# Layer 1's attention in groups of four heads, and six weight buffers instead of nine

## The chip, the cores and the metric

One core of a Trainium2 chip runs the whole program in one launch. The metric is device time in microseconds (us) of that core. Five engines work side by side, each through its own queue in order: TensorE (PE) for matrix products, VectorE (DVE), ScalarE (ACT), GpSimd (POOL), and SyncE (SP), which here issues the transfers from memory. PE writes its results to PSUM, of which the program uses eight banks: four under the name "acc" and four under the name "sc".

## The reference

A decoder of two layers over 256 tokens of 1024 numbers. Each layer adds an attention to its input and then a gated feed-forward part with a short convolution; all in float32, with a root-mean-square norm ahead of each.

```python
for i in range(DEPTH):                      # DEPTH = 2
    hn = rms_norm(h, norm_mix[i])
    if kind == 0:
        mix = moba_mixer(hn, a_w_qkv[j], a_w_o[j], cos_h, sin_h)
    elif kind == 1:
        mix = mla_mixer(hn, b_w_in[j], b_q_norm[j], b_w_uq[j], b_kv_norm[j], b_w_ukv[j], b_w_o[j], cos_r, sin_r)
...
    h = h + mix.astype(h.dtype)
    f = conv_ffn(rms_norm(h, norm_ffn[i]), ffn_w_gate[i], ffn_conv_w[i], ffn_conv_b[i], ffn_w_up[i], ffn_w_down[i])
    h = h + f.astype(h.dtype)
return rms_norm(h, norm_final)
```

Both attentions have 16 heads and are causal. With 256 tokens layer 0's is a plain softmax attention with 64 numbers a head. Layer 1's first makes small latents (384 and 256 numbers), and from them, for each head, a query and a key of 64 + 32 = 96 numbers (the last 32 rotated by position, and in the key shared by all heads) and a value of 64:

```python
s = jnp.einsum("bqhd,bkhd->bhqk", qi, k, preferred_element_type=jnp.float32) * scale
s = jnp.where(key_pos[None, :] <= qpos[:, None], s, NEG_INF)
p = jax.nn.softmax(s, axis=-1).astype(v.dtype)
return jnp.einsum("bhqk,bkhd->bqhd", p, v)
```

## The kernel before

**Weights.** All weights come in one stream of 186 units, in the order of use. A unit is up to 128 x 1152 numbers, mostly 128 x 1024. `load_unit` (L159) takes a room for the raw unit (pool `rawp`, five of them), has SP fetch it, and splits it into a high and a low part in two pieces of 512 columns: ACT casts `whi` (L173), DVE subtracts `wlo` = raw - whi (L174). The two parts lie in the pool `wp` (L125), which has nine buffers of each. `mm3` (L177) then makes each product of three matmuls, high x high, high x low, low x high (L178 to L180). A unit of 1024 columns feeds 24 matmuls of 256 columns. A buffer comes free when PE has done its last matmul with the unit; the cast for the unit nine further on waits for that, so nine is also how far ACT and DVE can work ahead of PE.

**Order.** Each engine works strictly in the order in which its instructions stand, and a program that builds the kernel sets that order: it may move instructions past each other according to when it expects buffers and results, so that the size of a pool changes the order too, at places that the code does not name.

**An attention in four groups.** Per group of four heads: the weights' products for q, k and v (the "filler", lists of small pieces of work that `run_fill` hands out), then for each head
- `products`: scores q x k into a bank "sc" (L279), two blocks of queries, of 128 and 256 keys;
- `exps`: DVE scales, masks and takes the row maxima from the bank (L293), ACT the exponentials with their sums (L296);
- `divide`: DVE's reciprocal (L304) and the division, on ACT (L307) or DVE (L309);
- `flip`: three transposes on PE into a bank "sc" (L316) and a copy `pT` of them;
- `values`: `pT` x v for a pair of heads, 64 columns of weights each, into a bank "sc" (L330), copied to `oh` on ACT (L332) and `ol` on DVE (L333).

**Layer 0** (`quads`, L351) does this for four heads at a time. Its heads have 2 x 32 rows, so the products of four heads run side by side in PE. In the stretch of a group stand the products and exponentials of its four heads, the transposes and values of the four before, and between them the filler for the next group, cut by shares of its length. Its tiles pb, pn, pT have four buffers each. The rotation of q and k is DVE's work (L569 to L571), q and k of a group before its products.

**Layer 1** (`run` and `slot`, L375 and L335) does it for two heads at a time, with a depth of two buffers: in slot p the values of pair p - 2, the products and softmax of pair p, the transposes of pair p - 1, with filler between. Here q is made with tokens in the rows (L776, and the rotation with DVE L251 and L253 and POOL L254), then flipped by four transposes per block of tokens (L807, with copies L808). The products have 96 rows. The divisions are DVE's, the copies `pT` ACT's for even heads and DVE's for odd ones.

**Feed-forward.** `ffn` (L419): for each pair of 128 columns, four units and 96 matmuls on PE; then `gate`, on DVE, ACT and POOL (from L438, ACT L442, gelu L447, POOL L448, to L451), beside the next pair's matmuls.

Of the kernel before, what the change touches and what calls it, by code (L numbers as in the profile page):

```python
# [10 lines left out]
F32 = mybir.dt.float32  # L11
# [5 lines left out]
P = 128  # L17
S = 256
NT = S // P
D = 1024  # L20
KD = D // P
H = 16
HD = 64
F = 2816
FC = F // P
QL, KVL, ROPE = 384, 256, 32
CQ, CKV = QL // P, KVL // P
DQK = HD + ROPE
G = 4
HG = H // G  # L30
# [90 lines left out]
def trunk(ctx: ExitStack, tc: tile.TileContext, xT, scalars, gfin, wstream, consts_in, out):  # L121
    nc = tc.nc
    const = ctx.enter_context(tc.tile_pool(name="const", bufs=1))
    rawp = ctx.enter_context(tc.tile_pool(name="rawp", bufs=5))
    wp = ctx.enter_context(tc.tile_pool(name="wp", bufs=9))  # L125
    act = ctx.enter_context(tc.tile_pool(name="act", bufs=1))
    sm = ctx.enter_context(tc.tile_pool(name="sm", bufs=4))
    ps = ctx.enter_context(tc.tile_pool(name="ps", bufs=1, space=PSUM))
# [62 lines left out]
    class SumSq:  # L191


        def __init__(self):
            self.acc = None
# [60 lines left out]
    def run_fill(fill, ns):  # L256
        while fill and ns > 0:
            cost, fn = fill.popleft()
            fn()
            ns -= cost  # L260
        return ns
# [3 lines left out]
    class Attention:  # L265


        def __init__(self, pool, scale, qT, kT, v, oh, ol, depth):
            self.pool, self.scale, self.qT, self.kT, self.v, self.oh, self.ol = pool, scale, qT, kT, v, oh, ol
            self.depth, self.sc, self.ex, self.pb, self.pT = depth, {}, {}, {}, {}  # L270

        def products(self, pair):
            sc = [ps.tile([P, 3 * P], F32, name="sc", bufs=4) for _ in pair]
            self.sc.update(zip(pair, sc))
            for t, (a, b) in enumerate(CUTS):
                parts = [list(zip(self.qT(n, t), self.kT(n, b - a))) for n in pair]
                for i in range(len(parts[0])):
                    for o, qk in zip(sc, parts):
                        nc.tensor.matmul(o[:, a:b], *qk[i], start=i == 0, stop=i == len(qk) - 1,  # L279
                                         skip_group_check=True)  # L280

        def softmax(self, n):
            self.exps(n)
            self.divide(n)

        def exps(self, n):
            sc = self.sc.pop(n)
# [12 lines left out]
        def divide(self, n):  # L300
            pb, rs = self.ex.pop(n)
            pn = self.pool.tile([P, 3 * P], F32, name="pn", bufs=self.depth)
            rc = sm.tile([P, NT], F32, name="rc")
            nc.vector.reciprocal(rc, rs)  # L304
            for t, (a, b) in enumerate(CUTS):
                if self.depth > 2:
                    nc.scalar.activation(pn[:, a:b], pb[:, a:b], AF.Copy, scale=rc[:, t:t + 1])  # L307
                else:
                    nc.vector.tensor_scalar(pn[:, a:b], pb[:, a:b], rc[:, t:t + 1], None, op0=ALU.mult)  # L309
            self.pb[n] = pn  # L310

        def flip(self, n):
            pb = self.pb.pop(n)
            pt = ps.tile([P, 3 * P], F32, name="sc", bufs=4)
            for b in range(3):
                nc.tensor.transpose(pt[:, b * P:(b + 1) * P], pb[:, b * P:(b + 1) * P], ident)  # L316
            pT = self.pool.tile([P, 3 * P], F32, name="pT", bufs=self.depth)
            if n % 2 == 0 or self.depth > 2:
                nc.scalar.copy(pT, pt)
            else:  # L320
                nc.vector.tensor_copy(pT, pt)
            self.pT[n] = pT

        def values(self, ns):
# [6 lines left out]
                                     start=t == 0, stop=t == NT - 1)  # L331
            nc.scalar.copy(self.oh[:, pr], o)  # L332
            nc.vector.tensor_sub(self.ol[:, pr], o, self.oh[:, pr].bitcast(F32))  # L333

        def slot(self, p, fill, ns):  # L335

            if p > 1:
                self.values((2 * p - 4, 2 * p - 3))
            if p < H // 2:
                pair = (2 * p, 2 * p + 1)  # L340
                self.products(pair)
                for n in pair:
                    self.softmax(n)
            left = run_fill(fill, ns * 0.4)
            if 0 < p <= H // 2:
                self.flip(2 * p - 2)
                left = run_fill(fill, left + ns * 0.2)
                self.flip(2 * p - 1)
                run_fill(fill, left + ns * 0.4)

        def quads(self, fill, next_fill):  # L351

            for g in range(G + 1):
# [17 lines left out]
                    self.values((n, n + 1))  # L371
                    run_fill(fill, ns * 0.1)
                run_fill(fill, 1e9)

        def run(self, fill, next_fill):  # L375
            for p in range(H // 2 + 2):
                if p and p % 2 == 0 and p < H // 2:
                    run_fill(fill, 1e9)
                    fill = next_fill(p // 2)
                slots = max(1, H // 2 + 1 - p) if p >= H // 2 - 2 else 2 - p % 2  # L380
                ns = sum(c for c, _ in fill) - (2600 if p >= H // 2 - 2 else 0)
                self.slot(p, fill, max(ns, 0) / slots)
            run_fill(fill, 1e9)

    def out_proj_fill(oh, ol, ks, accs):

# [171 lines left out]
    with tc.tile_pool(name="at0", bufs=1) as ap:  # L558
        ap.tile([P, 32], F32, name="pad")
        oh = ap.tile([P, KD, S], F32R, name="oh")  # L560
        ol = ap.tile([P, KD, S], F32R, name="ol")
# [64 lines left out]
        def group_fill(g):  # L626
            fill, us, box = deque(), [], {}

            def get(i):
                while len(us) <= i:  # L630
                    us.append(load_unit())
                return us[i]

            def qk(w, i, k):
                if i == 0 and k == 0:
                    box[w] = ps.tile([P, 2, S], F32, name="acc", bufs=4)
                wh, wl = get(2 * w + i)
                c = slice(k * P, (k + 1) * P)
                mm3(box[w][:, i], wh[:, c], wl[:, c], zh[:, k], zl[:, k], k == 0, k == KD - 1)
                if i == 1 and k == KD - 1:  # L640
                    evac_qk(g, w, box[w])

            def v(k, t):
                if k == 0 and t == 0:
                    box["v"] = ps.tile([P, NT, 256], F32, name="acc", bufs=4)
                mm_v(box["v"], get(4 + k // 4), k, t, k == 0)
                if k == KD - 1 and t == NT - 1:
                    evac_v(g, box["v"])

            for w in range(2):  # L650
                for i in range(2):
                    for k in range(KD):
                        fill.append((330, lambda w=w, i=i, k=k: qk(w, i, k)))
            for t in range(NT):
                for k in range(KD):
                    fill.append((330, lambda k=k, t=t: v(k, t)))
            return fill
# [11 lines left out]
        def v0(n, t):  # L669
            return vs[n // HG][:, t, n % HG]  # L670

        att = Attention(ap, HD ** -0.5, q0, k0, v0, oh, ol, HG)
        first_group()
        accs = []
        fill = group_fill(1)
        run_fill(fill, 5500)
        ks = {G - 1: range(4), G: range(4, KD - 2)}
# [10 lines left out]
    with tc.tile_pool(name="at1", bufs=1) as ap:  # L688
# [7 lines left out]
                c = slice(k * P, (k + 1) * P)  # L696
                mm3(dst, u[0][:, c], u[1][:, c], zh[:, k], zl[:, k], start and k == 0, k == KD - 1)

        tab = ap.tile([P, 3 * P], F32, name="pT", bufs=2)[:2 * ROPE, :S]
        nc.sync.dma_start(tab, consts_in[:2 * ROPE, CRT:])  # L700
        pkv = ps.tile([P, CKV, S], F32, name="acc", bufs=4)
        us = [load_unit() for _ in range(CKV)]
# [5 lines left out]
        for k in range(KD):  # L708
            c = slice(k * 2 * ROPE, (k + 1) * 2 * ROPE)
# [8 lines left out]
        for i in range(CQ):  # L718
            pq = ps.tile([P, S], F32, name="acc", bufs=4)
            mm_in(pq, load_unit(), range(KD), True)  # L720
            if i == 0:
                r2 = rstd_latent(ssk.columns(), KVL, r)
            if i == 1:
                R2 = rows_sb(r2)
                for j in range(CKV):
                    y = act.tile([P, S], F32, name="ssacc", bufs=2)
                    nc.vector.scalar_tensor_tensor(y, pkv[:, j], sc_in[:, GK + j:GK + j + 1], R2,
                                                   op0=ALU.mult, op1=ALU.mult)
                    nc.scalar.copy(ch[:, CQ + j], y)
                    nc.vector.tensor_sub(cl[:, CQ + j], y, ch[:, CQ + j].bitcast(F32))  # L730
                R0 = rows(r)
                tabR = ap.tile([P, 3 * P], F32, name="sb", bufs=2)[:2 * ROPE, :S]
                nc.vector.tensor_tensor(tabR, tab, R0[:2 * ROPE], op=ALU.mult)
                y = ap.tile([P, 3 * P], F32, name="pb", bufs=2)[:2 * ROPE, :S]
                nc.vector.tensor_tensor(y, pr[:2 * ROPE], tabR, op=ALU.mult)
                y2 = ap.tile([P, 3 * P], F32, name="pb", bufs=2)[:ROPE, :S]
                nc.scalar.copy(y2, y[ROPE:])
                nc.vector.tensor_tensor(kTs[0][HD:DQK], y[:ROPE, None, :].to_broadcast([ROPE, HG, S]),
                                        y2[:, None, :].to_broadcast([ROPE, HG, S]), op=ALU.add)
                nc.vector.tensor_copy(kTs[1][HD:DQK], kTs[0][HD:DQK])  # L740
            g = sc_in[:, GQ + i:GQ + i + 1]
            nc.scalar.activation(ch[:, i], pq, AF.Copy, scale=g)
            nc.vector.scalar_tensor_tensor(cl[:, i], pq, g, ch[:, i].bitcast(F32), op0=ALU.mult, op1=ALU.subtract)
            sqq = act.tile([P, 2, S], F32, name="sq", bufs=2)[:, 0]
            nc.scalar.activation(sqq, pq, AF.Square)
            ssq.add(sqq)
        oh = ap.tile([P, KD, S], F32R, name="oh")
# [76 lines left out]
        def v1(n, t):  # L824
            return vs[n // HG][:, t, n % HG]

        att = Attention(ap, DQK ** -0.5, q1, k1, v1, oh, ol, 2)
        ks, vv, qs, fl = group_fill(0)
        run_fill(deque(ks + vv), 1e9)
        r1 = rstd_latent(ssq.columns(), QL, r)  # L830
# [4 lines left out]
        accs = []  # L835
        fill = group_fill(1)
        for f in fl:
            run_fill(fill, 1000)
            f[1]()
        att.run(fill, lambda g: group_fill(g + 1) if g < G - 1 else out_proj_fill(oh, ol, range(KD - 2), accs))  # L840
        us = [load_unit() for _ in range(2)]
        zh, zl = new_z()
        ss = SumSq()
# [30 lines left out]
```

## Time and profile before

| | us |
|---|---|
| median of 3 runs | 590.43 |
| lowest and highest | 590.33, 590.66 |
| the profiled execution | 590.41 |
| its span, first to last instruction | 588.6 |
| PE busy | 575.8 |
| DVE busy | 421.2 |
| ACT busy | 355.9 |
| POOL busy | 50.6 |

The profile is one execution. A row of a timeline has the start in us from the span's start, the length, the engine, the line of the code, the operation, what it writes <- what it reads, its shape, and how many equal instructions stand in the row; in brackets, how long the engine stood idle before it, and what it had waited for. The length of PE's rows contains the way through the array; for the pace one reads start to start.

### The profile page before, as it was taken

How to read it: one execution, taken by the hardware profiler on the slowest of the kernel's cores; microseconds unless marked ns; L12 is line 12 of the kernel's file. 1: busy time of each engine (PE TensorE's matmuls, PEld its weight loads, DVE VectorE, ACT ScalarE, POOL GpSimd, SP SyncE). 2: the span in 40 equal slices, each digit the busy share in tenths (PEclk: the TensorE clock that was granted, in tenths of full speed). 3: DMA queues.
4: the chain of work that ended last, by engine and by line, in shares of the span. 5: the costliest groups of instructions: out<-in, count | busy, mean ns of one | idle time of the engine just before them, and what ended most of it. 6: DMA issues, size and time to landing. Idle time of an engine off the chain costs nothing.

```text
span 588.6 us, 12160 instructions
## 1 busy us (share of the span) xinstructions
PE 575.8 (98%) x4695; PEld 550.2 (93%) x4695; DVE 421.2 (72%) x908; ACT 355.9 (60%) x768; POOL 50.6 (9%) x47
## 2 busy tenths in 40 slices
PE   8998999999999999999999999999999999999995
PEld 7998999999999999999999888999999999988884
DVE  5898774595978778754488889658778778784403
ACT  6778778565656566544376677546657566573302
POOL 1000000001121211200002200000021211210001
PEclk9998999999999999999999999999999999999999
DMA  8667533535455656675636413255465656655101
GB/s 284 264 225 277 189 137 108 179 130 194 162 196 204 209 172 211 206 218 173 212 121 226 161 48 109 73 179 179 144 216 186 220 171 216 205 188 200 49 1 71
DMA packets 30074, 101.76 MB, mean 173 GB/s; under 512 B 3488, under 2 KB 4848, under 8 KB 30016
## 3 DMA queue, kind: packets, MB, share of 16 engines
q1 hardware_dynamic: 29744, 100.24, 50.5%
q8 instruction: 37, 0.61, 0.4%
q0 software_dynamic: 128, 0.48, 0.3%
q10 hardware_dynamic: 144, 0.26, 0.1%
q14 instruction: 21, 0.17, 0.1%
HBM read 99.92 MB, written 1.05 MB: 172 GB/s over the span
## 4 chain that ended last, share of the span: by engine, by line
PE 78%; issue 12%; DVE 4%; ACT 2%; DMA 2%; POOL 1%; SPq 0%; POOLq 0%; DVEq 0%; ACTq 0%
PE acc L178 19%; PE acc L179 19%; PE acc L180 19%; PE sc L179 5%; PE sc L178 5%; PE sc L180 5%; PE sc L279 3%; PE sc L330 2%; DVE wlo L174 2%; PE sc L316 2%; DMA raw<-in_wstream 2%; ACT whi L173 1%; PE sc L807 1%; ACT pb L296 0%; POOL r L216 0%
## 5 line engine op out<-in xcount | busy, mean ns | idle before, releaser
L174 DVE TENSOR_TENSOR wlo<-raw,whi 128x512 fp32r<-128x512 f32 (+1 forms) x371 | 239.9, 687 | 70.9 <-ACT whi L173 70.6
L173 ACT CAST whi<-raw 128x512 fp32r<-128x512 f32 (+1 forms) x371 | 209.9, 618 | 105.6 <-PE acc L180 43.4
L178 PE MATMUL acc<-zh,whi 128*128 128x256 f32 (+1 forms) x816 | 228.1, 280 | 0.3 <-ACT whi L173 0.3
L179 PE MATMUL acc<-zh,wlo 128*128 128x256 f32 (+1 forms) x816 | 226.5, 278 | 0.2 <-DVE wlo L174 0.2
L180 PE MATMUL acc<-zl,whi 128*128 128x256 f32 (+1 forms) x816 | 226.2, 277 | 0.0
L178 PEld LDWEIGHTS acc<-zh,whi 128*128 128x128 f32 (+1 forms) x816 | 153.5, 188 | 2.2 <-ACT whi L173 1.5
L179 PEld LDWEIGHTS acc<-zh,wlo 128*128 128x128 f32 (+1 forms) x816 | 153.5, 188 | 0.4 <-DVE wlo L174 0.4
L180 PEld LDWEIGHTS acc<-zl,whi 128*128 128x128 f32 (+1 forms) x816 | 153.3, 188 | 0.0
L448 POOL TENSOR_TENSOR gc<-gc,R 128x512 f32<-128x512 f32 x22 | 34.8, 1583 | 193.1 <-ACT gc L447 181.8
L178 PE MATMUL sc<-hh,whi 128*128 128x256 f32 x176 | 48.6, 276 | 0.0
L179 PE MATMUL sc<-hh,wlo 128*128 128x256 f32 x176 | 48.6, 276 | 0.0
L180 PE MATMUL sc<-hl,whi 128*128 128x256 f32 x176 | 48.6, 276 | 0.0
L450 ACT CAST hh<-gm 128x512 fp32r<-128x512 f32 x22 | 13.7, 621 | 44.1 <-DVE gm L449 44.1
L178 PE MATMUL acc<-oh,whi 128*128 128x256 f32 x128 | 38.0, 297 | 0.0
L179 PE MATMUL acc<-oh,wlo 128*128 128x256 f32 x128 | 36.0, 281 | 0.0
L180 PE MATMUL acc<-ol,whi 128*128 128x256 f32 x128 | 35.8, 280 | 0.0
L179 PE MATMUL sc<-whi,hl 128*128 128x512 f32 x88 | 34.6, 394 | 0.0
L178 PE MATMUL sc<-whi,hh 128*128 128x512 f32 x88 | 34.5, 393 | 0.0
L180 PE MATMUL sc<-wlo,hh 128*128 128x512 f32 x88 | 34.2, 389 | 0.0
L296 ACT ACTIVATE pb<-sb,nm 128x128 f32<-128x128 f32 x64 | 28.3, 445 | 8.5 <-DVE nm L293 8.5
L178 PEld LDWEIGHTS sc<-hh,whi 128*128 128x128 f32 x176 | 33.0, 188 | 0.0
L179 PEld LDWEIGHTS sc<-hh,wlo 128*128 128x128 f32 x176 | 33.0, 188 | 0.0
(143 smaller groups left out, 900.4 us busy)
## 6 DMA issues: line engine op xcount, KB each, us to landing
raw<-in_wstream SPq DMA_DIRECT2D x175, 512.0 KB, 4.1
raw<-in_wstream SPq DMA_DIRECT2D x13, 256.0 KB, 4.5
raw<-in_wstream SPq DMA_DIRECT2D x4, 576.0 KB, 3.7
h<-in_xT SPq DMA_DIRECT2D x8, 128.0 KB, 4.4
gl<-in_gfin SPq DMA_DIRECT2D x1, 512.0 KB, 3.7
out<-hn SPq DMA_DIRECT2D x1, 512.0 KB, 2.6
ropeR<-in_consts POOLq DMA_DIRECT2D x1, 384.0 KB, 4.4
out<-hn ACTq DMA_DIRECT2D x1, 256.0 KB, 2.7
```

The source lines that it names most:

```text
L173: nc.scalar.copy(hi[:, a:b], raw[:, a:b])
L174: nc.vector.tensor_sub(lo[:, a:b], raw[:, a:b], hi[:, a:b].bitcast(F32))
L178: nc.tensor.matmul(o, lh, rh, start=first, stop=False, skip_group_check=True)
L179: nc.tensor.matmul(o, ll, rh, start=False, stop=False, skip_group_check=True)
L180: nc.tensor.matmul(o, lh, rl, start=False, stop=last, skip_group_check=True)
L279: nc.tensor.matmul(o[:, a:b], *qk[i], start=i == 0, stop=i == len(qk) - 1, skip_group_check=True)
L296: nc.scalar.activation(pb[:, a:b], sb[:, a:b], AF.Exp, scale=-1.0, bias=nm[:, t:t + 1], accum_out=rs[:, t:t + 1])
L316: nc.tensor.transpose(pt[:, b * P:(b + 1) * P], pb[:, b * P:(b + 1) * P], ident)
L330: nc.tensor.matmul(o[j * HD:(j + 1) * HD, t * P:], self.v(n, t), pT[j][:, a:b], start=t == 0, stop=t == NT - 1)
L448: nc.gpsimd.tensor_tensor(gc, gc, Rb, op=ALU.mult)
L450: nc.scalar.copy(hh[:, f0:f0 + 2], gm)
L807: nc.tensor.transpose(pt[:DQK, i], st[g][:, t, i], ident)
```

## The change

`wp` goes from nine buffers to six. Layer 1's attention goes from `run` and `slot` to `quads`, so its products, exponentials, transposes, divisions and values come in fours as in layer 0, and its tiles pb, pn and pT get four buffers each, in the room of the three weight buffers. A new argument `on_act` keeps the divisions and copies on the engines that had them: ACT in layer 0, DVE (and ACT for even heads' copies) in layer 1. The filler of the last two stretches is the output product's first four and next two units instead of six in one list. `softmax`, `slot` and `run` go. Each engine has as many instructions as before. Line numbers of the new file are one higher up to the attention and lower behind it.

```diff
-    wp = ctx.enter_context(tc.tile_pool(name="wp", bufs=9))
+
+    wp = ctx.enter_context(tc.tile_pool(name="wp", bufs=6))
...
-        def __init__(self, pool, scale, qT, kT, v, oh, ol, depth):
+        def __init__(self, pool, scale, qT, kT, v, oh, ol, depth, on_act):
...
-                if self.depth > 2:
+                if self.on_act:
                     nc.scalar.activation(pn[:, a:b], pb[:, a:b], AF.Copy, scale=rc[:, t:t + 1])
...
-            if n % 2 == 0 or self.depth > 2:
+            if n % 2 == 0 or self.on_act:
                 nc.scalar.copy(pT, pt)
...
-        tab = ap.tile([P, 3 * P], F32, name="pT", bufs=2)[:2 * ROPE, :S]
+        tab = ap.tile([P, 3 * P], F32, name="pT", bufs=HG)[:2 * ROPE, :S]
...
-        att = Attention(ap, DQK ** -0.5, q1, k1, v1, oh, ol, 2)
+        att = Attention(ap, DQK ** -0.5, q1, k1, v1, oh, ol, HG, False)
...
-        att.run(fill, lambda g: group_fill(g + 1) if g < G - 1 else out_proj_fill(oh, ol, range(KD - 2), accs))
+        ks = {G - 1: range(4), G: range(4, KD - 2)}
+        att.quads(fill, lambda g: out_proj_fill(oh, ol, ks[g], accs) if g in ks else group_fill(g + 1))
```

The order moves at three places that matter below. **DVE in layer 0**, at the rotation of group 1's k (L569 to L571 before, L540 to L542 after; L174 and L175 are the subtractions of the weights, L304 and L301 the reciprocals of the softmax, L293 and L290 the reads of the score banks). Before:

```order
L304 RECIPROCAL rc<-rs 128x2 x3
L174 TENSOR_TENSOR wlo<-raw,whi 128x512 x2
L304 RECIPROCAL rc<-rs 128x2
L174 TENSOR_TENSOR wlo<-raw,whi 128x512 x3
L569 TENSOR_TENSOR rt_610<-acc,ropeR 128x512
L570 TENSOR_TENSOR rt_611<-acc,ropeR 128x512
L174 TENSOR_TENSOR wlo<-raw,whi 128x512
L571 TENSOR_TENSOR kT<-rt_610,rt_611 128x512
L174 TENSOR_TENSOR wlo<-raw,whi 128x512 x11
L293 ISA sb,nm<-sc,cst 128x128
```

The same place after, on DVE:

```order
L301 RECIPROCAL rc<-rs 128x2 x3
L175 TENSOR_TENSOR wlo<-raw,whi 128x512 x2
L301 RECIPROCAL rc<-rs 128x2
L175 TENSOR_TENSOR wlo<-raw,whi 128x512
L540 TENSOR_TENSOR rt_610<-acc,ropeR 128x512
L541 TENSOR_TENSOR rt_611<-acc,ropeR 128x512
L175 TENSOR_TENSOR wlo<-raw,whi 128x512
L542 TENSOR_TENSOR kT<-rt_610,rt_611 128x512
L175 TENSOR_TENSOR wlo<-raw,whi 128x512 x7
L290 ISA sb,nm<-sc,cst 128x128
```

Two subtractions went from in front of the two rope products to behind them, and behind kT stand seven subtractions ahead of the next reads of the score banks instead of eleven.

**ACT, a little ahead of that place**, with the casts of weights (L173, L174 after) in front of the exponentials of the first four heads (L296, L293 after; L581 and L552 scale group 0's v). Before:

```order
L581 ACTIVATE v<-acc,r 128x256 x2
L173 CAST whi<-raw 128x512 x12
L296 ACTIVATE pb,rs<-sb,nm 128x128
L296 ACTIVATE pb,rs<-sb,nm 128x256
L296 ACTIVATE pb,rs<-sb,nm 128x128
```

After, on ACT:

```order
L552 ACTIVATE v<-acc,r 128x256 x2
L174 CAST whi<-raw 128x512 x10
L293 ACTIVATE pb,rs<-sb,nm 128x128
L293 ACTIVATE pb,rs<-sb,nm 128x256
L293 ACTIVATE pb,rs<-sb,nm 128x128
```

One unit's two casts left the place in front of the exponentials; they stand behind the divisions now.

**PE in layer 1**, where pairs of value products (L330, L327 after; the row with 64x256 is for 128 rows of keys by two heads) meet the products of scores (L279, L280 after) and the filler. One of three such places before:

```order
L807 MATMUL sc<-cst,qn 96x128 x4
L330 MATMUL sc<-pT,v 64x256
L180 MATMUL acc<-wlo,ch 128x384
L178 MATMUL acc<-whi,ch 128x384
L279 MATMUL sc<-kT_4140,qT 128x128 x2
L279 MATMUL sc<-kT_4140,qT 128x256
L330 MATMUL sc<-pT,v 64x256
L330 MATMUL sc<-pT,v 64x128 x2
L279 MATMUL sc<-kT_4140,qT 128x256
L179 MATMUL acc<-whi,cl 128x384
```

Where the first values of layer 1 stand after, on PE:

```order
L179 MATMUL acc<-whi,ch 128x256
L180 MATMUL acc<-whi,cl 128x256
L181 MATMUL acc<-wlo,ch 128x256
L327 MATMUL sc<-pT,v 64x256 x2
L327 MATMUL sc<-pT,v 64x128 x2
L778 MATMUL sc<-cst,qn 96x128 x4
L280 MATMUL sc<-kT_4139,qT 128x128 x2
L179 MATMUL acc<-whi,ch 128x384
```

The four value rows of a pair stand together now, at all eight places of layer 1; before, five of the eight did. (The profile counts each score and value product of the order as two instructions.) In the feed-forward parts, and wherever else in the program the two orders are not cut by these places, the rows are the same, with each weight unit's conversion at a place where that of the unit three later stood.

## Rows read from the trace of the kernel before

**Rows 1.** The page: span, busy time of PE, and granted clock in 40 slices.
```profile
span 588.6 us, 12160 instructions
...
PE 575.8 (98%) x4695; PEld 550.2 (93%) x4695; DVE 421.2 (72%) x908; ACT 355.9 (60%) x768; POOL 50.6 (9%) x47
...
PEclk9998999999999999999999999999999999999999
```

**Rows 2.** Waits of PE over the program: line, releaser, total us, times, longest.
```profile
PE sc L279 <- DVE kT L571: 1.9, 1, 1.9
...
PE sc L807 <- POOL qn L254: 0.9, 1, 0.9
```

**Rows 3.** PE's timeline in layer 0, around group 1's products.
```profile
43.30 0.28 PE L179 MATMUL acc<-whi,zl 128*128 128x256 f32 x1
43.41 0.28 PE L180 MATMUL acc<-wlo,zh 128*128 128x256 f32 x1
45.54 2.05 PE L279 MATMUL sc<-kT,qT 32*128 32x128 f32 x32 [1.85 <-DVE kT L571]
...
52.12 0.28 PE L180 MATMUL acc<-zl,whi 128*128 128x256 f32 x1
52.80 0.41 PE L316 MATMUL sc<-cst,pn 128*128 128x128 f32 x2 [0.41 <-DVE nm L293]
```

**Rows 4.** Stretches: length, busy us by engine (instructions), granted clock, DMA share, GB/s.
```profile
43.10:46.50 3.40, 1.55 (x30) 1.34 (x32) 3.40 (x6) 3.40 (x7) 0.00 (x0) 1.00 0.85 302
46.50:49.90 3.40, 3.40 (x23) 2.74 (x18) 3.40 (x7) 3.05 (x8) 0.00 (x0) 0.50 0.68 230
```

**Rows 5.** DVE's timeline at the same place.
```profile
41.21 1.87 DVE L174 TENSOR_TENSOR wlo<-raw,whi 128x512 fp32r<-128x512 f32 x3
43.00 0.68 DVE L569 TENSOR_TENSOR rt<-acc,ropeR 128x512 f32<-128x512 f32 x1
43.60 0.68 DVE L570 TENSOR_TENSOR rt<-acc,ropeR 128x512 f32<-128x512 f32 x1
...
44.80 0.68 DVE L571 TENSOR_TENSOR kT<-rt,rt 128x512 f32<-128x512 f32 x1
45.40 6.70 DVE L174 TENSOR_TENSOR wlo<-raw,whi 128x512 fp32r<-128x512 f32 x11
52.02 0.28 DVE L293 CUSTOM_DVE_ANT_0 sb<-sc,cst 128x128 f32<-128x128 f32 x1
```

**Rows 6.** ACT's timeline before it: last casts, first exponential, divisions.
```profile
36.04 1.14 ACT L173 CAST whi<-raw 128x512 fp32r<-128x512 f32 x2 [0.27 <-DMA raw<-in_wstream]
37.09 0.40 ACT L296 ACTIVATE pb<-sb,nm 128x128 f32<-128x128 f32 x1
...
40.61 2.87 ACT L307 ACTIVATE pn<-pb,rc 128x128 f32<-128x128 f32 x8
```

**Rows 7.** DVE's timeline at the start of layer 1's attention.
```profile
328.98 0.68 DVE L174 TENSOR_TENSOR wlo<-raw,whi 128x512 fp32r<-128x512 f32 x1
```

**Rows 8.** PE's timeline in layer 1, a pair of values cut in two.
```profile
366.45 0.65 PE L330 MATMUL sc<-pT,v 128*64 128x256 f32 x2
...
367.27 0.36 PE L178 MATMUL acc<-oh,whi 128*128 128x256 f32 x1
...
369.36 0.47 PE L179 MATMUL acc<-oh,wlo 128*128 128x256 f32 x1
369.67 0.28 PE L180 MATMUL acc<-ol,whi 128*128 128x256 f32 x1
```

**Rows 9.** PE's timeline in layer 1, a pair of values in one piece.
```profile
346.96 0.87 PE L330 MATMUL sc<-pT,v 128*64 128x256 f32 x8
...
349.30 0.28 PE L179 MATMUL acc<-ch,wlo 128*128 128x256 f32 x1
```

**Rows 10.** Feed-forward of layer 0: DVE's subtractions at the first gate, and PE.
```profile
150.84 1.88 DVE L174 TENSOR_TENSOR wlo<-raw,whi 128x512 fp32r<-128x512 f32 x3
...
156.01 0.28 PE L178 MATMUL acc<-zh,whi 128*128 128x256 f32 x1
```

More of the change, by code (lines that the diff above doesn't have):

```diff
@@ L265, in trunk @@
     class Attention:
-        def __init__(self, pool, scale, qT, kT, v, oh, ol, depth):
+        def __init__(self, pool, scale, qT, kT, v, oh, ol, depth, on_act):
             self.pool, self.scale, self.qT, self.kT, self.v, self.oh, self.ol = pool, scale, qT, kT, v, oh, ol
-            self.depth, self.sc, self.ex, self.pb, self.pT = depth, {}, {}, {}, {}
+            self.depth, self.on_act, self.sc, self.ex, self.pb, self.pT = depth, on_act, {}, {}, {}, {}
         def products(self, pair):
@@ L280, in products @@
                                          skip_group_check=True)
-        def softmax(self, n):
-            self.exps(n)
-            self.divide(n)
         def exps(self, n):
@@ L333, in values @@
             nc.vector.tensor_sub(self.ol[:, pr], o, self.oh[:, pr].bitcast(F32))
[L335 to L349, printed above, removed]
         def quads(self, fill, next_fill):
@@ L373, in quads @@
                 run_fill(fill, 1e9)
[L375 to L383, printed above, removed]
     def out_proj_fill(oh, ol, ks, accs):
@@ L670, in v0 @@
             return vs[n // HG][:, t, n % HG]
-        att = Attention(ap, HD ** -0.5, q0, k0, v0, oh, ol, HG)
+        att = Attention(ap, HD ** -0.5, q0, k0, v0, oh, ol, HG, True)
         first_group()
@@ L733, in trunk @@
                 nc.vector.tensor_tensor(tabR, tab, R0[:2 * ROPE], op=ALU.mult)
-                y = ap.tile([P, 3 * P], F32, name="pb", bufs=2)[:2 * ROPE, :S]
+                y = ap.tile([P, 3 * P], F32, name="pb", bufs=HG)[:2 * ROPE, :S]
                 nc.vector.tensor_tensor(y, pr[:2 * ROPE], tabR, op=ALU.mult)
-                y2 = ap.tile([P, 3 * P], F32, name="pb", bufs=2)[:ROPE, :S]
+                y2 = ap.tile([P, 3 * P], F32, name="pb", bufs=HG)[:ROPE, :S]
                 nc.scalar.copy(y2, y[ROPE:])
```

## Prediction

> **What bounds the kernel now.** I read the first two parts of the page, then the waits of TensorE (PE), then its timeline wherever a wait or a dip showed. PE is busy for 575.8 of 588.6 us and its granted clock stands at nine tenths or more in all but one slice of the page's row [rows 1], so only two things can move the end: time in which PE does nothing, and time that PE spends changing from one kind of work to another. The waits are few: 1.9 us in layer 0's attention for VectorE's (DVE's) kT, 0.9 us at the start of layer 1's for a rope sum on GpSimd (POOL) [rows 2]. DVE and ScalarE (ACT) have slack; they count only where PE waits for one of their results. The profiled execution took 590.41 us (span 588.6, 1.8 around it), the median of the other runs 590.43, so a sum made against the span holds for the median.
>
> **Part 1: layer 0, which the diff does not name but whose order moves.** With six instead of nine weight buffers, ACT and DVE may convert three units less ahead of PE, so conversions that stood in front of other work there now stand behind it.
>
> In group 1 PE finishes its filler with the matmul that starts at 43.41, at 0.11 per matmul, and its score products start only at 45.54: 2.0 us of nothing [rows 3]. Right behind it the granted clock is 0.50 (the 1.2 GHz level) for 3.4 us, after 3.4 us in which PE was busy for 1.55 [rows 4]. What PE waits for is kT of L571, which starts at 44.80, behind three subtractions at 41.21, two rope products at 43.00 and 43.60, and a subtraction more [rows 5]. In the new order one subtraction stands ahead of the two products instead of three, and ACT's casts of the third unit (36.04, after a wait for its transfer) stand behind the exponentials instead of in front of them [rows 6]. Step by step: the exponentials start at 36.0 instead of 37.09, so ACT's eight divisions end at 42.4 instead of 43.5; the cast of the third unit follows, its first half at 43.0; DVE has long done L569 and L570 and now waits for that half, since its subtraction stands between L570 and L571. Subtraction 0.6, kT 0.68: ready at 44.35, PE starts at 44.4. **Gain 1.1 us**, PE's gap 0.9 in place of 2.0. Bounds: 0, if a transfer holds a cast up, and 2.0, if the gap closes wholly. Two subtractions fewer at 0.6 would give 1.2 by themselves, so 1.1 is near the middle of what the rows say.
>
> The clock: 3.4 us at half speed cost 1.7 us of work. The nearest row for a gap half as long is the 0.9 us wait at 330.7 [rows 2], behind which no clock falls in the page's row [rows 1]. So I take the fall as gone: **gain 1.7**, bounds 0 and 1.7.
>
> Then PE's first transpose of that group starts at 52.80, where the matmul before it would have let it start at 52.23; it waits for a score bank, which DVE's L293 reads from 52.02 on, behind eleven subtractions [rows 3, 5]. Seven stand there now. From kT's end at 44.35 they take 4.2 us, so the first head's bank is free at about 49.2 (two reads, 0.7). PE needs it after the product block (2.0 long here, about 1.5 without the slow clock) and 30 matmuls of 0.12: 44.4 + 1.5 + 3.6 = 49.5. **Gain 0.6**, bounds 0 and 0.6. In all 3.4 us for layer 0.
>
> **Part 2: the way into layer 1.** The rope sum for which PE waits 0.9 us comes behind a subtraction of 0.6 at 328.98 that now stands later [rows 7], so the sum is ready 0.6 us sooner. Against it, the new order puts two matmuls of 384 columns (about 0.17 each) behind the transposes of q instead of ahead of them, and the products of the fourth head need a copy of q on ACT that comes no sooner. Net **0.2**, bounds 0 and 0.6.
>
> **Part 3: layer 1's attention.** No instruction is added or taken away on PE: 64 products, 48 transposes, 64 value matmuls stay as they were, and the divisions stay on DVE. What changes is which of them are neighbours. Before, in three of the eight pairs the value matmuls (64 columns of weights) are cut in two by score products (96 rows) and filler. From the first value matmul at 366.45 to the matmul at 369.67 lie 8 values, 8 products and 2 matmuls of 0.12: 3.22 - 0.24 = 2.98 us [rows 8]. The same 16 in one piece, from 346.96 to 349.30 with one matmul: 2.34 - 0.12 = 2.22 us [rows 9]. So a cut pair costs 0.76 us more, in time that PE is busy: the page shows no wait there, it is the change of shape. The pairs at 340.25 and 352.92 are cut in the same way (their stretches differ by a few hundredths). In the new order all eight value blocks stand whole. **Gain 3 x 0.76 = 2.3 us.** A change between value block and transposes of q, which is new at two places, I price like that to products. Bounds: 2.3, and 0.3 if PE then waits for the score banks (second rival).
>
> **Costed at nothing, with its cover: the feed-forward parts.** Three buffers fewer are three units, at 24 matmuls of 0.11 [rows 3] some 8 us of lead. The conversions and everything behind them keep their order there; each position is simply filled by a unit three earlier. So I matched units and matmuls by count and took for each unit the end of the subtraction that is now three units further on. The smallest lead in layer 0 is at the first gate: the subtraction that ends at 152.72 will be that of the unit which PE starts at 156.01, 3.3 us ahead [rows 10]; the same place in layer 1 differs by a tenth, and everywhere else the count gives more. Were that cover gone, each late subtraction would cost up to its 0.68 us, at each of 22 gates.
>
> **Sum.** 3.4 + 0.2 + 2.3 = 5.9 us: 590.4 - 5.9 = **584.5 us**.
>
> **Rivals.**
> *The clock still falls.* For it: 0.9 us of gap followed by a block of 32-row products is less work than what surrounded the 0.9 us at 330.7. Then 584.5 + 1.7 = 586.2.
> *PE waits for the score banks in layer 1.* Products of four heads take all four "sc" banks at once, where pairs took two, and the next transposes need one back. In groups 2 and 3 DVE has up to four subtractions of 0.6 ahead of the reads that free the banks, and the filler between products and transposes of group 2 is four matmuls only. For a price I take the one such wait in the trace, the 0.6 us at 52.80 [rows 3], at one to three groups, and at most 2 us in all: 585.1 to 586.5. Against it: layer 0 uses the same shape and its other groups show no wait of PE [rows 2]. The Trainium skill (Perfetto Trace Analysis, Matmuls) says that independent groups of matmuls should rotate through PSUM banks so that the evacuation of one overlaps the next; that speaks against taking all four at once, and by it this rival is the outcome.
> *Layer 0 gains nothing.* If the rope products start late for another reason (transfers, the pool's order), only parts 2 and 3 stay: 587.9. Against it: at 43.00 DVE comes straight from a subtraction, with no idle time [rows 5].
> *Slower.* The conversions miss their cover in the feed-forward parts. It decides from the point where a conversion ends 5 us later against PE than counted; a late subtraction of 0.68 at 20 gates would be 13.6 us: 584.5 + 13.6 = 598. Against it: the leads above.
>
> **How the numbers follow.** The forecast has 0.56 (583.5 to 585.1), the clock 0.15, the banks 0.13, layer 0 without gain 0.07, slower 0.06; 0.03 for a mixture of the middle three that ends within 0.2% (1.2 us) of 590.4, about the least that a measurement of this kernel can tell from no change. Faster by more than that: 0.91; same 0.03; slower 0.06. The range takes in the forecast and the first three rivals: 583.4, with the gap in layer 0 closed as well (0.9) and something over, to 587.9.
>
> **What would show it.** Right: PE's gap before the products of group 1 in layer 0 near 0.9 us and no second slice with a reduced clock but the last; the first transpose behind it without idle time; eight whole value blocks of 0.8 us in layer 1; no wait of PE for casts or subtractions in the feed-forward parts. Wrong: a clock of 0.5 after 44 us, PE waiting for L290 or L293 (the reads of the banks and the exponentials) in layer 1, or waits on whi and wlo after 130 us.

## The result and the profile after

The changed kernel takes **584.73 us** (median of 3 runs, 584.54 to 584.84) against 590.43 before: a ratio of 0.9894, 95% interval 0.9876 to 0.9913, 5.7 us less. The forecast was 584.5. Its profiled execution has a span of 583.1 us against 588.6, which is 5.5 us less.

First the page of the kernel after: busy time of TensorE (PE) and the granted clock in 40 slices, which answer to [rows 1].

```profile
PE 572.3 (98%) x4695; PEld 548.5 (94%) x4695; DVE 421.1 (72%) x908; ACT 355.6 (61%) x768; POOL 49.3 (8%) x47
...
PEclk9999999999999999999999999999999999999998
```

The number of PE's instructions is that of before, its busy time 3.5 us shorter, and the reduced slice in layer 0 is gone. Now all of PE's waits, to be read beside [rows 2].

```profile
engine line waited for: us in total, times, longest us
PE sc L155 <- DVE whi L136: 1.5, 1, 1.5
PE sc L778 <- POOL qn L255: 0.8, 1, 0.8
PE sc L280 <- DVE kT L542: 0.6, 1, 0.6
PE acc L179 <- ACT whi L174: 0.4, 1, 0.4
PE acc L180 <- DVE wlo L175: 0.2, 1, 0.2
```

The wait for kT is 0.6 instead of 1.9 us, and no line names the reads of the score banks (L290) or the exponentials (L293), in either layer. The 0.8 us for the rope sum at the start of layer 1 is still there.

**Layer 0, group 1.** PE's timeline, beside [rows 3].

```profile
43.65 0.28 PE L181 MATMUL acc<-wlo,zh 128*128 128x256 f32 x1
44.51 1.59 PE L280 MATMUL sc<-kT,qT 32*128 32x128 f32 x32 [0.58 <-DVE kT L542]
46.03 0.38 PE L179 MATMUL acc<-zh,whi 128*128 128x256 f32 x1
...
49.44 0.28 PE L181 MATMUL acc<-zl,whi 128*128 128x256 f32 x1
49.56 0.49 PE L313 MATMUL sc<-cst,pn 128*128 128x128 f32 x3
```

From the last filler matmul to the first transpose it is 5.91 us; in [rows 3] it was 9.39. The transposes follow the matmul ahead of them without idle time. VectorE (DVE) and ScalarE (ACT) at the same place, beside [rows 5, 6]:

```profile
41.53 0.68 DVE L541 TENSOR_TENSOR rt<-acc,ropeR 128x512 f32<-128x512 f32 x1
43.16 0.69 DVE L175 TENSOR_TENSOR wlo<-raw,whi 128x512 fp32r<-128x512 f32 x1 [0.95 <-ACT whi L174]
43.77 0.68 DVE L542 TENSOR_TENSOR kT<-rt,rt 128x512 f32<-128x512 f32 x1
44.37 4.30 DVE L175 TENSOR_TENSOR wlo<-raw,whi 128x512 fp32r<-128x512 f32 x7
48.58 0.28 DVE L290 CUSTOM_DVE_ANT_0 sb<-sc,cst 128x128 f32<-128x128 f32 x1
...
39.75 2.87 ACT L304 ACTIVATE pn<-pb,rc 128x128 f32<-128x128 f32 x8
42.52 3.73 ACT L174 CAST whi<-raw 128x512 fp32r<-128x512 f32 x7
```

This is the chain that the prediction built by hand: ACT's divisions end at 42.5, the cast follows, DVE has waited 0.95 us for its first half, then come subtraction and sum. Seven subtractions stand ahead of the reads, and the reads start 1.0 us before PE needs a bank.

**Layer 1's attention.** PE's timeline with the first two value blocks and what follows them, beside [rows 8, 9].

```profile
345.16 0.87 PE L327 MATMUL sc<-pT,v 128*64 128x256 f32 x8
...
346.87 0.87 PE L327 MATMUL sc<-pT,v 128*64 128x256 f32 x8
347.67 0.64 PE L778 MATMUL sc<-cst,qn 128*96 128x128 f32 x4
```

All eight blocks stand whole, 0.80 us each from start to next start.

**Where the 5.5 us come from.** PE runs the same 4,695 instructions, so a matmul outside of layer 1's attention can be compared by its number, its start after less its start before. After is 0.24 late at the end of group 0 (all of it arises in the first 16 us, where the variants of after, with the same order there, differ as much among themselves), 3.34 early at the end of layer 0's attention and unchanged through its whole feed-forward part up to 313.9, 3.22 early at 327.92, just behind the wait for the rope sum, where both orders have done the same matmuls, and 5.53 early from 404.5 to the end. So layer 0's attention gave 3.58, the entry of layer 1 took back 0.12, layer 1's attention gave 2.31, both feed-forward parts nothing.

The smallest lead in the feed-forward part of layer 0, beside [rows 10]:

```profile
147.54 1.88 DVE L175 TENSOR_TENSOR wlo<-raw,whi 128x512 fp32r<-128x512 f32 x3
...
152.67 0.28 PE L179 MATMUL acc<-zh,whi 128*128 128x256 f32 x1
```

The three subtractions end at 149.42, and PE starts on that unit at 152.67: 3.25 us, where 3.3 were counted.

### The profile page after: what moved, and what is told of

It reads as the page before. It is cut to its first block, busy times and chain, and to the rows that moved or that the text cites. A ratio compares the mean times of both kernels' runs of the same rounds, so it can differ in the third digit from the quotient of the medians.

```text
span 583.1 us, 12151 instructions
## 1 busy us (share of the span) xinstructions
PE 572.3 (98%) x4695; PEld 548.5 (94%) x4695; DVE 421.1 (72%) x908; ACT 355.6 (61%) x768; POOL 49.3 (8%) x47
## 4 chain that ended last, share of the span: by engine, by line
PE 81%; issue 10%; ACT 2%; DVE 2%; DMA 2%; POOL 1%; SPq 1%; POOLq 0%; ACTq 0%; DVEq 0%
PE acc L179 20%; PE acc L180 20%; PE acc L181 20%; PE sc L181 5%; PE sc L180 5%; PE sc L179 5%; PE sc L280 3%; PE sc L327 2%; PE sc L313 2%; DMA h<-in_xT 1%; ACT whi L174 1%; DMA raw<-in_wstream 1%; PE sc L778 1%; DVE wlo L175 1%; ACT pb L293 1%
## 5 line engine op out<-in xcount | busy, mean ns | idle before, releaser
L175 DVE TENSOR_TENSOR wlo<-raw,whi 128x512 fp32r<-128x512 f32 (+1 forms) x371 | 239.9, 687 | 75.8 <-ACT whi L174 75.5
L174 ACT CAST whi<-raw 128x512 fp32r<-128x512 f32 (+1 forms) x371 | 209.9, 618 | 109.8 <-PE acc L181 36.4
L293 ACT ACTIVATE pb<-sb,nm 128x128 f32<-128x128 f32 x64 | 28.3, 443 | 8.1 <-DVE nm L290 8.1
```

Source lines behind the costliest of these rows:

```text
L174: nc.scalar.copy(hi[:, a:b], raw[:, a:b])
L175: nc.vector.tensor_sub(lo[:, a:b], raw[:, a:b], hi[:, a:b].bitcast(F32))
L293: nc.scalar.activation(pb[:, a:b], sb[:, a:b], AF.Exp, scale=-1.0, bias=nm[:, t:t + 1], accum_out=rs[:, t:t + 1])
```

## The experiments

The question was which of the change's two halves gave what, and whether the three terms of layer 0, the price of a cut block and the cover of the feed-forward parts are what the prediction took them for. The median of the kernel before lay between 590.43 and 591.51 from one group of runs to another, so ratios to it are given as well. Its 46 single times beside the experiments fall into two groups: 28 lie from 590.43 to 591.51, 18 from 591.85 to 593.45. The profiled execution (590.41) and the three of the result lie with the lower group; no profile shows one of the upper, and what makes it longer is open.

**before_six.** Only the number of weight buffers is changed.

```
-    wp = ctx.enter_context(tc.tile_pool(name="wp", bufs=9))
+    wp = ctx.enter_context(tc.tile_pool(name="wp", bufs=6))
```

> The kernel before with six weight buffers instead of nine and nothing else: layer 1's attention stays in pairs. Theory (layer 0's gain comes from the order alone, by the smaller lead of the conversions): the gap before the score products of layer 0's group 1 shrinks from 2.0 to about 0.6 us, no half clock behind it, no wait at the first transpose; 3.3 us less than before, 587.1 us; three of eight value blocks in layer 1 stay cut. Rival (layer 0's gain hangs on the other edits, the new groups of four): 590.4 us.

Measured: 587.24 us, ratio 0.9929 (0.9915 to 0.9943). PE's products in its timeline:

```profile
44.28 1.59 PE L279 MATMUL sc<-kT,qT 32*128 32x128 f32 x32 [0.57 <-DVE kT L571]
```

The gap is that of after, the clock is 1.00 behind it, and layer 1 has its three cut blocks. So layer 0's gain comes from the buffers alone, and the order that they bring is that of after: one subtraction ahead of the rope products, seven ahead of the reads. What after has beyond it is layer 1's: 587.24 - 584.73 = 2.5 us between the medians, 2.3 between the profiled executions.

**before_eight.** The same line with `bufs=8`.

> The kernel before with eight weight buffers. Nine instead of eleven subtractions stand ahead of the reads of the score banks in layer 0's group 1, but still three ahead of the rope products. Theory (the three terms of layer 0 are separate): the gap of 2.0 us and the half clock behind it stay, the wait of 0.6 us at the first transpose goes; 589.8 us. Rival (one term: fewer buffers help as a whole, each a third): 589.3 us with the gap smaller.

Measured: 589.79 us, ratio 0.9974 (0.9963 to 0.9985). The time is the theory's, the mechanism isn't. PE's and DVE's timeline in the profiled execution, and below them the stretch from 46.00 (length, busy us by engine with instructions, granted clock, DMA share, GB/s):

```profile
46.42 1.59 PE L279 MATMUL sc<-kT,qT 32*128 32x128 f32 x32 [1.96 <-DVE kT L571]
52.49 0.52 PE L316 MATMUL sc<-cst,pn 128*128 128x128 f32 x3 [0.85 <-DVE nm L293]
...
46.28 5.50 DVE L174 TENSOR_TENSOR wlo<-raw,whi 128x512 fp32r<-128x512 f32 x9
51.70 0.28 DVE L293 CUSTOM_DVE_ANT_0 sb<-sc,cst 128x128 f32<-128x128 f32 x1
...
46.00:50.00 4.00, 3.58 (x49) 3.23 (x50) 4.00 (x8) 3.60 (x8) 0.00 (x0) 1.00 0.81 294
```

The gap is 2 us as before, yet the clock stays at 1.00, and PE waits 0.85 us for the score bank in spite of two subtractions fewer. So the half clock and the wait for the bank are not two terms that add: PE's slow matmuls and DVE's subtractions run beside each other, and the transposes start at the later of the two. In the kernel before, DVE's row of subtractions runs without a break from 45.40 to the reads at 52.02 [rows 5], so the bank comes free at the same time with a fast PE, and the half clock cost nothing in that execution: even behind it PE still waited 0.41 us for the bank [rows 3].

**after_seven.** The kernel after with `bufs=7`: three subtractions ahead of the rope products again, seven ahead of the reads.

> The kernel after with seven weight buffers instead of six: three subtractions instead of one stand ahead of the rope products in layer 0's group 1, layer 1 as after. Theory (a gap of 2.0 us is followed by half clock): the gap is 2.0 again, 1.3 us more, and the clock falls to 0.5 for some 3.4 us, 1.7 us more; 587.7 us. Rival (the half clock has another cause than the gap): 586.0 us, granted clock 1.0 behind the gap. Rival (the extra buffer costs nothing): 584.7 us.

Measured: 587.07 us, ratio 0.9924 (0.9908 to 0.9941), and the six times fall into two groups: 587.74, 587.76, 587.61, and 586.14, 586.53, 585.79. The profiled execution, PE's timeline and the stretch behind the gap:

```profile
45.95 2.13 PE L280 MATMUL sc<-kT,qT 32*128 32x128 f32 x32 [2.16 <-DVE kT L542]
...
48.60 0.41 PE L181 MATMUL acc<-zl,whi 128*128 128x256 f32 x1
48.82 0.41 PE L179 MATMUL acc<-zh,whi 128*128 128x256 f32 x1
...
46.00:49.40 3.40, 3.40 (x38) 2.68 (x39) 3.40 (x6) 2.86 (x6) 0.00 (x0) 0.63 0.89 302
```

A matmul takes 0.21 us there instead of 0.11, the mean clock of the stretch is 0.63, and the bank is free in time, so that nothing hides it: from the products to the first transpose it is 6.64 us, in after 5.05, a cost of 1.59. That is also the distance of the two groups of times, and each group lies where one of the first two cases expected it. So a gap of 2 us may or may not be followed by the 1.2 GHz level: it was in the profiled executions of before and after_seven and wasn't in that of before_eight. The gap of 0.6 us was followed by it in none of the eight profiles with such a gap. That one and the same program does both is read from the six times of after_seven; no profile shows an execution of its lower group. Their mean granted clocks speak for it: 0.994, 0.994 and 0.995 in the upper group, 0.996 three times in the lower. The Trainium skill (TensorE: Matmul & The Clock Gate, What's actually happening) says that the chip's watch on TensorE's activity runs free and doesn't start with the kernel. The two groups agree with it, but no run here shows it.

**after_five.** The kernel after with `bufs=5`.

> The kernel after with five weight buffers. Theory: one subtraction fewer ahead of the rope products again, so the gap of 0.6 us before the score products of layer 0's group 1 closes, and the smallest lead of the conversions in the feed-forward parts falls from 3.8 us by one unit of 24 matmuls (2.7 us) to about 1.1, still no wait: 584.1 us. Rival (the cover of the feed-forward parts ends here): TensorE waits for casts and subtractions at the first gates of both layers, at 0.7 us each, 585 to 590 us.

Measured: 584.41 us, ratio 0.9881 (0.9863 to 0.9900). The time fits, the reason for it falls: the gap is still 0.6 us. DVE's and ACT's timelines:

```profile
40.29 0.68 DVE L541 TENSOR_TENSOR rt<-acc,ropeR 128x512 f32<-128x512 f32 x1
42.91 0.69 DVE L175 TENSOR_TENSOR wlo<-raw,whi 128x512 fp32r<-128x512 f32 x1 [1.94 <-ACT whi L174]
...
39.49 2.87 ACT L304 ACTIVATE pn<-pb,rc 128x128 f32<-128x128 f32 x8
42.27 3.72 ACT L174 CAST whi<-raw 128x512 fp32r<-128x512 f32 x7
```

The rope products come 1.2 us sooner and DVE then waits 1.94 instead of 0.95 us: what is late is the cast behind ACT's divisions. The feed-forward parts show no wait.

**after_four.** The kernel after with `bufs=4`.

> The kernel after with four weight buffers. Each pair of units in the feed-forward parts can then be converted only when the pair but one before it is done, 48 matmuls (5.4 us) later than with six. The smallest lead measured with six is 3.8 us at 158.11. Theory (the slower case decides at 3.8 us): the first gate of each layer is missed by 1.6 us and the later ones are not, 584.4 + 3.2 = 587.6 us. Rival (missed again at each gate, since the gates' own work stands ahead of the casts): 0.7 us at 20 of 22 gates, 598 us. Rival (the conversions move up and nothing waits): 584.4 us.

Measured: 588.78 us, ratio 0.9961 (0.9939 to 0.9984). PE waits once in each layer:

```profile
148.90 0.38 PE L180 MATMUL sc<-zh,wlo 128*128 128x256 f32 x1 [1.22 <-DVE wlo L175]
...
425.18 0.38 PE L180 MATMUL sc<-zh,wlo 128*128 128x256 f32 x1 [1.28 <-DVE wlo L175]
```

Each costs 1.5 us by the same matmul in after; another 0.6 is lost at layer 1's first products (303 to 309). The place is two pairs of units ahead of the one expected, and the expected lead of 3.8 us was not the smallest, which is 3.25 at 152.67. So the cover ends between five and four buffers, and what its end costs is one wait per layer, not one at every gate: a late start moves PE's later needs by as much. Eight of the ten times lie from 588.07 to 589.02, two at 592.56 and 594.09, which no profile shows. By the median the kernel isn't slower than before even with four buffers.

**after_cut.** The kernel after with six value blocks of layer 1 cut behind their first matmul.

```
...
                     nc.tensor.matmul(o[j * HD:(j + 1) * HD, t * P:], self.v(n, t), pT[j][:, a:b],
                                      start=t == 0, stop=t == NT - 1)
+                    if t + j == 0 and not self.on_act:
+                        run_fill(fill, 1)
...
```

> The kernel after, with the value block of six of the eight pairs of layer 1 cut after its first matmul by three or six matmuls of filler, the same work in another order. Theory (a cut costs the change of shape, whatever stands in the cut): 6 x 0.76 = 4.6 us more than after, 589.3 us, without any wait of TensorE. Rival (the cost in the kernel before came from the score products of 96 rows in the cut, not from the cut): two changes between filler and values more per cut, 0.1 each, 6 x 0.2 = 1.2 us, 585.9 us.

Measured: 588.87 us, ratio 0.9956 (0.9941 to 0.9971), 4.1 us more than after, and no new wait. One cut block in PE's timeline:

```profile
345.02 0.65 PE L327 MATMUL sc<-pT,v 128*64 128x256 f32 x2
345.60 0.39 PE L179 MATMUL acc<-whi,ch 128*128 128x256 f32 x1
...
346.51 0.86 PE L327 MATMUL sc<-pT,v 128*64 128x256 f32 x6
347.30 0.64 PE L780 MATMUL sc<-cst,qn 128*96 128x128 f32 x4
```

The two instructions take 0.58 us and the six 0.79 (start to next start), together 1.37 where a whole block takes 0.80; the two changes of shape more in between make up the rest. At the end of layer 1's attention the kernel is 4.5 us behind after by the same matmul, 6 x 0.76; 0.5 of that comes back in the output projection, whose matmuls took 113 instead of 118 ns here (more on that below). The cut costs, not what stands in it.

**after_entry.** The rope sums of group 0 of layer 1 go to DVE.

```
...
-                    rope(st[g][:, t, :, HD:], pv[:, :, HD:], ropeR[:, t], HG, ap)
+                    rope(st[g][:, t, :, HD:], pv[:, :, HD:], ropeR[:, t], HG, ap, nc.vector if g == 0 else None)
...
```

> The kernel after, with the rope sums of layer 1's group 0 on VectorE instead of GpSimd. Theory: the 0.8 us that TensorE waits for the sum at layer 1's entry shrinks to 0.2, 584.1 us. Rival: the order built from it puts the eight score products of group 1 straight in front of the transposes, so that TensorE waits for a score bank there, 0.6 us or more, and nothing is gained: 584.7 us.

Measured: 584.79 us, but spread from 583.71 to 586.83 over six runs; ratio 0.9893 (0.9874 to 0.9912), which can't be told from after. PE's wait in the profiled execution:

```profile
326.56 0.61 PE L778 MATMUL sc<-cst,qn 128*96 128x128 f32 x4 [0.52 <-DVE qn L255]
```

0.5 us instead of 0.8, and no wait for a bank: neither case as expected, and what spread the times stayed open.

**after_join.** The blocks of two pairs are put behind each other, in both layers.

```
                 for n in old[::2]:
                     self.values((n, n + 1))
-                    run_fill(fill, ns * 0.1)
+                run_fill(fill, ns * 0.2)
```

> The kernel after, with the value blocks of two pairs put behind each other in both layers, eight blocks of sixteen instead of sixteen of eight. If a change of shape costs what the blocks of after show (0.10 into the block, 0.13 in it, 0.11 out of it), each join saves 0.33 us, 8 x 0.33 = 2.6 us, 582.1 us. Rival (the second pair then waits for its transposed exponentials or its bank): 584.7 us.

Measured: 593.12 us, ratio 1.0024 (1.0013 to 1.0035): 8 us slower than after, with no wait that after hasn't. In layer 0's attention four joins gain 1.2 us by the same matmul, near the 1.3 that were expected. The loss lies in the feed-forward parts. The stretch from 160 to 260 us, which is feed-forward in all three, of after, of after_join and, below, of after_join_part:

```profile
160.00:260.00 100.00, 100.00 (x885) 100.00 (x884) 77.37 (x136) 60.45 (x111) 12.51 (x9) 1.00 0.66 203
...
160.00:260.00 100.00, 100.00 (x851) 100.00 (x850) 74.96 (x132) 58.43 (x109) 12.36 (x8) 1.00 0.61 193
...
160.00:260.00 100.00, 100.00 (x885) 100.00 (x884) 77.40 (x136) 60.45 (x111) 12.47 (x8) 1.00 0.66 204
```

PE is busy throughout at full clock and does 851 instead of 885 matmuls in the same 100 us: 118 instead of 113 ns for each, the same instruction on the same operands.

**after_join_part.** As after_join, but the last two blocks of each layer stay apart.

```
                 for n in old[::2]:
                     self.values((n, n + 1))
-                    run_fill(fill, ns * 0.1)
+                    if g == G:
+                        run_fill(fill, ns * 0.1)
+                if g < G:
+                    run_fill(fill, ns * 0.2)
```

> As after_join, but the last two value blocks of each layer, ahead of the output projection and the feed-forward part, stay apart as in after. In after_join the matmuls of 256 columns took 118 ns instead of 113 in both feed-forward parts, 11 us in all, without any wait. Theory (which of the two steps a long run of matmuls takes is set by the form of the last blocks ahead of it): 113 ns again, and six joins at 0.33 us: 582.7 us. Rival (any joined block leaves the slower step behind for good): 584.7 - 2.0 + 11 = 594 us.

Measured: 583.85 us, ratio 0.9878 (0.9861 to 0.9894). The step is 113 ns again (the third line above). Against the 584.81 of after in the same group of runs (after_again, below) the six joins gave 1.0 us, not 2.0. By the same matmuls in the traces it is 1.3: 0.28 each in layer 0, about 0.16 each in layer 1, where the order built also cuts the score products behind a joined block at another place; the profiled execution lost 0.45 of that in its start.

**after_k_pool.** The sum that makes kT of group 1 in layer 0 goes to GpSimd; nothing else moves.

```
...
-            evac_rope(dst[g], pq)
+            evac_rope(dst[g], pq, nc.gpsimd if g == 1 and which else None)
```

> The kernel after, with the sum that makes kT of layer 0's group 1 on GpSimd instead of VectorE; no other instruction moves against another. Theory (TensorE's rest of a gap, 0.6 us, is the cast and the subtraction that stand ahead of the sum on VectorE): the sum starts when L541 ends, some 42.2, takes 1.6 us as the sums of the gates do, and TensorE starts at 43.9 instead of 44.5: 584.1 us. Rival (GpSimd is later than that): 584.7 us or more.

Measured: 584.36 us, ratio 0.9888 (0.9873 to 0.9903). GpSimd's and PE's timelines:

```profile
42.47 1.30 POOL L542 TENSOR_TENSOR kT<-rt,rt 128x512 f32<-128x512 f32 x1 [20.14 <-DVE rt L541]
...
43.83 0.28 PE L181 MATMUL acc<-wlo,zh 128*128 128x256 f32 x1
44.04 1.59 PE L280 MATMUL sc<-kT,qT 32*128 32x128 f32 x32
```

The sum no longer queues behind the cast and the subtraction, and PE's gap is closed. The gain over after in the same group of runs is 0.45 us between the medians, and the two sets of four times overlap by 0.1.

**after_join_k_pool and after_again.** Both of the last two edits together, and the kernel after once more beside them.

> after_join_part and after_k_pool together. If both theories hold: 582.7 - 0.6 = 582.1 us, less than both kernels. If the slower step of the matmuls stays: 593 us.

> The kernel after once more, beside the three others: 584.7 us; half clock nowhere but at the end, a gap of 0.6 us in layer 0's group 1, 113 ns per matmul in the feed-forward parts.

Measured: 583.03 us (582.93 to 583.15), ratio 0.9865 (0.9851 to 0.9880), for the two edits together, and 584.81, ratio 0.9896 (0.9882 to 0.9911), for after, whose profile shows the gap of 0.6 us, the full clock and the 113 ns again. So the combination beats both kernels: 1.8 us less than after, where the two edits one by one gave 0.45 and 0.96; at least their sum is there, and what the rest is stayed open.

## Why the prediction was right, step by step

**The gap in layer 0** was put at 0.9 us and a gain of 1.1. From 43.41 to 45.54 it was 2.13 from start to start in [rows 3], in after from 43.65 to 44.51 it is 0.86: a gain of 1.27. The chain through ACT's divisions, the cast, the subtraction and the sum came out as timed by hand, and after_five and after_k_pool confirm what ends it: taking a subtraction away ahead of it changes nothing, taking the sum out of the queue closes the gap.

**Clock and score bank** were put at 1.7 + 0.6 = 2.3 us. From the products to the transposes it was 7.26 us in [rows 3] and is 5.05, a gain of 2.21. The sum was right and its parts were not: before_eight shows that the wait for the bank grows when the half clock is absent, so in the kernel before the bank set the time by itself, and the half clock was hidden. What the change had to do for the 2.2 us was both, to shorten the row of subtractions and the gap. The rival that kept the half clock was priced rightly all the same, since in the new order nothing hides it: after_seven puts it at 1.6.

**The entry of layer 1** was put at a gain of 0.2; it was a loss of 0.1, which is there ahead of the wait already, at the transposes of L236 around 317.7 (0.12). At the wait nothing is won: the sum is ready 0.3 us sooner, not 0.6, as the scale that it needs (DVE's L227, behind GpSimd's L217) came 0.17 later and the subtraction that stays has 576 columns; and PE comes to it 0.34 sooner with two matmuls fewer ahead; so the wait stays at 0.8 and the two matmuls follow it:

```profile
325.94 0.34 PE L180 MATMUL acc<-whi,cl 128*128 128x384 f32 x1
327.09 0.64 PE L778 MATMUL sc<-cst,qn 128*96 128x128 f32 x4 [0.81 <-POOL qn L255]
```

**The value blocks of layer 1** were put at 3 x 0.76 = 2.3 us; measured 2.31 for the whole attention of layer 1, other new neighbours included, and after_cut repeats the price in the other direction.

**The feed-forward parts** were costed at nothing with a smallest lead of 3.3 us; measured nothing, with 3.25. The slower rival exists, but two buffers further on, and its price of 13.6 us was far too high: after_four pays 1.5 per layer and 0.6 between them.

**The rival of the score banks** didn't come about: PE's waits name no bank in layer 1. It was near: at 339.77 PE's transposes start where the second read of the first bank, from 339.25 on for 0.42 us, has ended 0.1 us earlier. The two rows, PE's and DVE's:

```profile
339.77 0.51 PE L313 MATMUL sc<-cst,pn 128*128 128x128 f32 x3
...
339.25 0.42 DVE L290 CUSTOM_DVE_ANT_0 sb<-sc,cst 128x256 f32<-128x256 f32 x1
```

The Trainium skill (Perfetto Trace Analysis, Matmuls) says that independent groups of matmuls should rotate through the banks, so that emptying one goes on beside the next group. That taking all four banks at once would therefore cost a wait was the prediction's reading of it; the trace shows none.

The 5.9 us of the sum against 5.5 in the spans and 5.7 between the medians is thus 0.2 more in layer 0's attention, 0.3 less at the entry, and 0.24 lost in the first 16 us of this execution. What the prediction had no case for is the length of the step in the feed-forward parts, which stayed at 113 ns through the change but could have gone the other way.

## What to carry to other kernels

A smaller ring of buffers isn't only a loss of lead: where the program that sets the order fills it as far as it goes, it also keeps work that isn't urgent out of the queues ahead of work that is, and the lead can be counted from the trace before, unit by unit. Two delays that end in the same wait don't add; take the later one, and ask for each what is next when it goes. On a busy PE, read the start-to-start step of its matmuls by shape and by stretch: changes of shape and the step itself move time that no list of waits shows.

## What the runs showed of the hardware

**Two steps for one matmul.** A matmul of 256 columns with its own weights takes 113 or 118 ns from start to start, at full clock and without a wait, and keeps to one of the two over hundreds of instructions, over 1,400 in layer 0's feed-forward part; it changed over where other shapes came between. In before and after both feed-forward parts run at 113 and the output projections ahead of them at 118; in after_join it is the other way round, at 34 matmuls less in 100 us, 11 us over both layers. after_join and after_join_part differ only in whether the last value blocks of a layer are joined, so the order of shapes ahead of a long stretch can set its step. What in it does is open.

**The clock after a gap.** 2 us of idle PE were followed by the 1.2 GHz level in two of three profiles (before and after_seven, not before_eight) and, as its times are read, in three of six executions of after_seven, at 1.6 us each; 0.6 us were not in any of eight profiles.

**Changes of shape.** A block of eight value instructions (64 columns of weights) takes 0.80 us whole and 1.37 cut into two and six, before what the neighbours pay; joined, it saves some 0.28 us per join in layer 0.
